# Attention scores of two heads as two 64-row products in two PSUM banks instead of one zero-padded 128-row product

## The chip, the cores and the metric

One core of a Trainium2 chip. The metric is the device time of one execution in microseconds. Before the change the median of three runs is 1158.2 us (1157.85 to 1158.86).

## What is computed

Three transformer blocks on one sequence of 256 tokens, width 1024, batch 1, all in float32. Layer 0 mixes tokens by two kinds of attention, layer 1 by a third; both end in a SwiGLU feed-forward. The third block (a gated linear recurrence) is not touched. Every score below is a product over a head dimension of 64:

```python
# layer 0, stick-breaking attention: 8 heads, each with its own key
z = einsum('bqhd,bshd->bhqs', qb, k) * scale
log_keep = where(past, log_sigmoid(-z), 0.0)
suffix = cumsum(log_keep, axis=3, reverse=True) - log_keep
w = where(past, exp(log_sigmoid(z) + suffix), 0.0)
# layer 0, gathered attention: 4 index heads pick 64 keys for each query, 8 heads share one key
logits = einsum('bqhe,bse->bhqs', qib, k_idx) * IDX_DIM ** -0.5
score = einsum('bhqs,bqh->bqs', relu(logits), wb)
_, sel = top_k(score, topk)
s = einsum('bqhd,bqkd->bhqk', qb, k[sel]) * d ** -0.5      # then softmax, times v[sel]
# layer 1, differential attention: 8 heads, two score maps each
s = einsum('bqhcd,bshcd->bhcqs', qb, k) * d ** -0.5
p = softmax(where(causal, s, -inf))
a = p[:, :, 0] - lam * p[:, :, 1]
```

## The kernel before

Activations lie transposed, features on the 128 partitions and tokens along the free axis. Weights stream from HBM by SyncE in slabs of 1 MB. ACT rounds each slab to a high part, `whi`, DVE subtracts for a low part, `wlo`, and a projection product is three PE products of 128x256 (`mm3`). The first seven slabs of layer 0 stay whole and are multiplied as float32.

No instruction is issued where it is written. The class `Plan` records every operation (`record`), `order` (line 259) lays them out on a modelled clock, with a cost for each from `cost` (line 181), a due time from the place in the text plus a bias, and buffers from fixed sets (`BUFS`); `issue` then emits them (all at line 433, so the profile shows that one line). Each engine executes its list in that order. Attention is written as generators, of which `spin` takes a step between projections, so that the planner mixes their operations into the projections.

Two heads share a 128-partition tile, one on rows 0 to 63, one on rows 64 to 127. To get both heads' scores in one product, one operand is padded: the key (layers 0's shared key in `kz_d` and `kz_i`, layer 1's in `kzt`) or the query (stick-breaking, `qz`) is laid out twice as wide, with the other head's rows zero, after a memset by GpSimd (POOL). One product over all 128 rows then gives a bank of both heads' scores, side by side:

```python
T.matmul(o, qi[:, c * S + t * 128:c * S + t * 128 + 128], two(kz_i)[:, :, :nk], start=True, stop=True)
```

`t` is the block of 128 queries; it sees `nk` = 128 or 256 keys, so such a product has 256 or 512 columns. There are 4 in `gen_topk` (index scores), 8 in `gen_dsa`, 8 in `gen_sb` (512 and 256 columns), 16 in `gen_diff`. A mask is added by a bfloat16 product with the identity (`identb`). Softmax (`softmax_pair`), exponentials and relu read the bank; probabilities are transposed by PE (`ps_t`) and multiplied by the values (`ps_o`). In `gen_sb` the values' products write 64 rows for each of two heads, on the two halves of the array's columns. `do_sb` copies queries from PSUM into `qz`, the loop over `h` in layer 1 writes q and k by additions (rotary embedding).

Of the kernel before, what the change touches and what calls it, by code (L numbers as in the profile page):

```python
# [59 lines left out]
BUFS = {'w4': 19, 'w2': 5, 'w1': 11, 'sm': 16, 'stage': 3, 'mst': 3, 'whi': 6, 'wlo': 6}  # L60
# [45 lines left out]
class Plan:  # L106
# [74 lines left out]
    def cost(self, eng, op, writes, reads):  # L181
# [255 lines left out]
def kernel(ctx, tc, io, out):  # L437
# [261 lines left out]

    def root(dst, eps, src=None):  # L700
# [253 lines left out]
    kz_t = w4("kzt")  # L954
    kz_d = kz_t[:, 0:512]
    kz_i = kz_t[:, 512:1024]
    G.memset(kz_t[:, 0:1024], 0.0)
# [6 lines left out]
    for a, kz, r0 in ((0, kz_d, 0), (1, kz_i, 64)):  # L964
        for b in range(2):
            V.tensor_add(kz[b * 64:b * 64 + 64, b * S:(b + 1) * S], t1[r0:r0 + 64, 0, :], t2[r0:r0 + 64, 0, :])
# [18 lines left out]
    def gen_topk():  # L985
        for t in range(2):
            nk = 128 * (t + 1)
            s = bias[:, t, :]
            for c in range(2):
                ps = bank("ps_i")  # L990
                o = two(ps[:, :2 * nk])
                T.matmul(o, qi[:, c * S + t * 128:c * S + t * 128 + 128], two(kz_i)[:, :, :nk], start=True, stop=True)
                r = two(w2("rl")[:, :2 * nk])
                A.activation(r, o, AF.Relu)
                for a in range(2):
                    if c == 0 and a == 0:
                        V.tensor_scalar(s[:, :nk], r[:, 0, :], wix[:, t, 0:1], 0.0, op0=ALU.mult, op1=ALU.add)
                    else:
                        V.scalar_tensor_tensor(s[:, :nk], r[:, a, :], wix[:, t, 2 * c + a:2 * c + a + 1], s[:, :nk],
# [48 lines left out]
    def gen_dsa():  # L1048
        for t in range(2):
            nk = 128 * (t + 1)  # L1050
            PT = [w4c(f"pt{t}{i}", S) for i in range(t + 1)]
            for j in range(4):
                ps = bank("ps_i")
                o = two(ps[:, :2 * nk])
                T.matmul(o, qd[j // 2][:, (j % 2) * S + t * 128:(j % 2) * S + t * 128 + 128], two(kz_d)[:, :, :nk],
                         start=True, stop=False)
                T.matmul(o, identb, biasb[:, t, None, :nk].to_broadcast([128, 2, nk]), start=False, stop=True)
                e = two(w2("e"))
                ls = softmax_pair(e, o, nk)
                for a in range(2):  # L1060
                    if a < EACT:
                        A.activation(e[:, a, :nk], e[:, a, :nk], AF.Copy, scale=ls[:, a:a + 1])
                    else:
                        V.tensor_scalar(e[:, a, :nk], e[:, a, :nk], ls[:, a:a + 1], None, op0=ALU.mult)
                for st in range(t + 1):
                    pt = bank("ps_t")
                    for a in range(2):
                        T.transpose(pt[:, a * 128:a * 128 + 128], e[:, a, st * 128:st * 128 + 128], ident)
                    A.activation(PT[st].rearrange("p j (a q) -> p a j q", a=2)[:, :, j, :], two(pt[:, :256]), AF.Copy)
                yield  # L1070
# [11 lines left out]
    qz = [w4("qz0"), w4("qz1")]  # L1082
    ks = w4c("ksb", S)
    for i in range(2):
        G.memset(qz[i], 0.0)

    def do_sb():
        for i in range(2):
            ps = two(next_pair())
            for c in range(2):  # L1090
                for a in range(2):
                    A.activation(qz[i][a * 64:a * 64 + 64, c * 512 + a * S:c * 512 + a * S + S], ps[a * 64:a * 64 + 64, c, :],
                                 AF.Copy, scale=0.125)
# [30 lines left out]
    def gen_sb():  # L1124
        for j in range(4):
            qzj = two(qz[j // 2][:, (j % 2) * 512:(j % 2) * 512 + 512])
            za, zb = bank("ps_z"), bank("ps_z")
# [743 lines left out]
```

## Time and profile before

| | |
|---|---|
| median of three runs | 1158.2 us |
| the profiled execution | 1161.21 us, span 1159.4 us |
| PE, DVE, ACT, POOL busy | 1127.6, 912.1, 723.1, 12.4 us |
| PE instructions | 8787 products, 8787 weight loads |
| mean granted PE clock | 0.99 |
| read from HBM | 229.81 MB |

The profile takes one execution apart. Busy time is the union of an engine's instructions; for the PE the ends are modelled, since products overlap in its pipeline, so prices are taken from the distance between starts. In a row's form, 128*128 says how many rows and columns of the array the instruction uses, 128x256 the output. A float32 product shows as two instructions. "Idle before" and the name behind it tell what released the engine. PEld is the weight load that belongs to a product.

### The profile page before, as it was taken

The page shows a single profiled execution, that of the slowest core. Times are in us where ns is not written, and L with a number is a line of the kernel's source. Part 1 is how long each engine was busy: PE and PEld are TensorE (multiplying, and loading weights), DVE is VectorE, ACT ScalarE, POOL GpSimd, SP SyncE. Part 2 cuts the span into 40 slices and gives each one's busy share as a digit, 9 for nine tenths or more (in the row PEclk, how much of TensorE's full clock was granted, in tenths as well). Part 3 has the DMA queues.
Part 4 walks back from the last instruction along what each step waited for, and adds up shares of the span by engine and source line. Part 5 has one row for each costly group of instructions (what it writes and reads, how often), then busy time and mean ns, then how long its engine had stood idle before and what let it go on. Part 6 is the DMA issues. An engine that isn't in the chain of part 4 may idle for free.

```text
span 1159.4 us, 21967 instructions
## 1 busy us (share of the span) xinstructions
PE 1127.6 (97%) x8787; PEld 1079.3 (93%) x8787; DVE 912.1 (79%) x1764; ACT 723.1 (62%) x1314; POOL 12.4 (1%) x18
## 2 busy tenths in 40 slices
PE   5999999999999899999999999999999999999997
PEld 4886799999998779999999999999999999999996
DVE  6799899888989899995557696996579886767652
ACT  3558677444459987764445377876757765555541
POOL 1010000000010000000000000000000000000000
PEclk9999999999999999999999999999999998999998
DMA  9938748998983244585554524344433434555441
GB/s 349 411 125 316 258 146 326 331 338 308 338 327 121 87 168 146 200 309 183 178 200 168 198 82 173 120 165 156 180 110 124 168 110 146 207 187 184 169 164 37
DMA packets 42247, 232.27 MB, mean 200 GB/s; under 512 B 4641, under 2 KB 6177, under 8 KB 24097
## 3 DMA queue, kind: packets, MB, share of 16 engines
q1 hardware_dynamic: 42144, 230.87, 54.9%
q8 instruction: 69, 1.13, 0.4%
q14 instruction: 34, 0.27, 0.1%
HBM read 229.81 MB, written 1.05 MB: 199 GB/s over the span
## 4 chain that ended last, share of the span: by engine, by line
PE 82%; DVE 9%; ACT 5%; DMA 3%; issue 1%; SPq 0%; DVEq 0%; ACTq 0%
PE pa L433 82%; DVE w L433 5%; ACT w L433 4%; DMA mst<-in_wmod_dram 2%; DVE wlo L433 2%; DVE mst L433 1%; ACT whi L433 1%; DVE sm L433 1%; DMA w<-in_pos_dram 1%; DMA w<-in_xT_dram 1%; DVE stage L433 0%; SPq L433 0%; ACT sm L433 0%; DVE mw L433 0%; DVEq L1867 0%
## 5 line engine op out<-in xcount | busy, mean ns | idle before, releaser
L433 PE MATMUL pa<-w,whi 128*128 128x256 f32 (+4 forms) x5104 | 920.3, 288 | 9.3 <-DMA whi<-in_w_dram 7.4
L433 PEld LDWEIGHTS pa<-w,whi 128*128 128x128 f32 x5104 | 771.2, 190 | 18.5 <-ACT w L433 6.7
L433 PE MATMUL pa<-w,wlo 128*128 128x256 f32 (+3 forms) x2608 | 665.7, 290 | 2.2 <-DVE wlo L433 2.2
L433 ACT ACTIVATE whi<-stage 128x1024 fp32r<-128x1024 f32 (+1 forms) x330 | 338.7, 1041 | 254.8 <-PE pa L433 226.6
L433 PEld LDWEIGHTS pa<-w,wlo 128*128 128x128 f32 x2608 | 467.2, 190 | 9.0 <-DVE wlo L433 4.0
L433 DVE TENSOR_TENSOR wlo<-stage,whi 128x1024 fp32r<-128x1024 f32 (+1 forms) x330 | 392.8, 1201 | 93.1 <-ACT whi L433 90.8
L433 ACT ACTIVATE w<-w 128x256 fp32r<-128x256 f32 (+9 forms) x257 | 117.1, 468 | 71.6 <-DVE w L433 68.0
L433 DVE TENSOR_TENSOR w<-w,w 128x256 fp32r<-128x256 f32 (+6 forms) x323 | 144.8, 465 | 10.9 <-ACT w L433 9.0
L433 ACT ACTIVATE w<-pa 128x256 f32<-128x256 f32 (+12 forms) x298 | 108.0, 390 | 47.1 <-PE pa L433 41.4
L433 DVE SCALAR_TENSOR_TENSOR mst<-mst,scb 128x1024 f32<-128x1024 f32 x90 | 108.7, 1221 | 9.2 <-DMA mst<-in_wmod_dram 8.9
L433 DVE TENSOR_TENSOR w<-w,pa 128x256 f32<-128x256 f32 (+2 forms) x146 | 58.7, 418 | 56.7 <-PE pa L433 52.0
L432 ACT ACT_TABLE_LOAD x61 | 78.3, 1283 | 1.8 <-PEq L1861 0.7
L433 PE MATMUL pa<-w,w 128*128 128x128 f32 (+8 forms) x340 | 68.6, 334 | 3.0 <-issue 1.6
L433 PEld LDWEIGHTS pa<-w,w 128*128 128x128 f32 (+4 forms) x340 | 41.9, 174 | 13.1 <-issue 7.1
L433 PE MATMUL pa<-cst,w 128*128 128x1 f32 (+4 forms) x236 | 38.8, 255 | 3.3 <-ACT w L433 3.3
L433 PEld LDWEIGHTS pa<-cst,w 128*128 128x128 f32 (+2 forms) x236 | 29.0, 158 | 10.0 <-ACT w L433 6.1
L433 PE MATMUL pa<-w 128*128 128x128 f32 x240 | 34.6, 275 | 0.0
L433 PE MATMUL pa<-whi,w 128*128 128x512 f32 x96 | 32.6, 423 | 0.0
L433 PEld LDWEIGHTS pa<-w 128*128 128x128 f32 x240 | 31.3, 191 | 0.0
L433 DVE SCALAR_TENSOR_TENSOR w<-pa,vec,w 128x256 f32<-128x256 f32 (+1 forms) x48 | 23.1, 483 | 6.6 <-PE pa L433 5.7
L433 DVE SCALAR_TENSOR_TENSOR w<-pa,mod,w 128x256 f32<-128x256 f32 x32 | 15.0, 481 | 14.8 <-PE pa L433 14.8
L433 DVE COPY_PREDICATED w<-msk,pa 128x512 f32<-128x512 uint8 x28 | 20.5, 737 | 3.9 <-PE pa L433 3.8
(144 smaller groups left out, 478.1 us busy)
## 6 DMA issues: line engine op xcount, KB each, us to landing
mst<-in_wmod_dram SPq DMA_DIRECT2D x90, 512.0 KB, 5.5
stage<-in_wgu_dram SPq DMA_DIRECT2D x44, 1024.0 KB, 5.0
stage<-in_wi_dram SPq DMA_DIRECT2D x36, 1024.0 KB, 4.8
stage<-in_wup_dram SPq DMA_DIRECT2D x22, 1024.0 KB, 4.8
stage<-in_wd_dram SPq DMA_DIRECT2D x24, 896.0 KB, 4.5
stage<-in_w_dram SPq DMA_DIRECT2D x15, 1024.0 KB, 6.7
stage<-in_wo_dram SPq DMA_DIRECT2D x12, 1024.0 KB, 4.8
stage<-in_wd_dram SPq DMA_DIRECT2D x12, 1024.0 KB, 5.4
```

The lines of the kernel that those rows point to most:

```text
L432: self.nc.scalar.preload_act_table_set(tables[i])
L433: fn(*[real(a) for a in args], **{k: real(a) for k, a in kw.items()})
```

## The change

The padding goes. Query and key of a pair of heads lie on the same rows, and a helper issues one product of 64 rows for each head, into two banks, for each of two column parts `c`; a bank now holds two scores of heads on the same rows. `gen_diff` treats two heads together: its bank holds the same score map of heads `h` and `h + 1`. The padded tiles and their memsets are dropped, `w2` gets a sixth buffer, and the planner's cost of a float32 product of 64 rows is halved.

```diff
-BUFS = {'w4': 19, 'w2': 5, 'w1': 11, 'sm': 16, 'stage': 3, 'mst': 3, 'whi': 6, 'wlo': 6}
+BUFS = {'w4': 19, 'w2': 6, 'w1': 11, 'sm': 16, 'stage': 3, 'mst': 3, 'whi': 6, 'wlo': 6}
...
-                return max(214.0, 4 * n / 2.4 + 5)
+                return max(214.0, 4 * n / 2.4 + 5) / (2 if reads[0].shape[0] == 64 else 1)
...
+    def scores(o, c, left, right, stop=False):
+
+        for a in range(2):
+            r = slice(a * 64, a * 64 + 64)
+            T.matmul(o[a][:, c, :], left[r], right[r], start=c == 0, stop=stop, skip_group_check=True)
...
-    kz_t = w4("kzt")
-    kz_d = kz_t[:, 0:512]
-    kz_i = kz_t[:, 512:1024]
-    G.memset(kz_t[:, 0:1024], 0.0)
+    kz_d, kz_i = w2("kd2")[:, :S], w2("ki2")[:, :S]
...
             for c in range(2):
-                ps = bank("ps_i")
-                o = two(ps[:, :2 * nk])
-                T.matmul(o, qi[:, c * S + t * 128:c * S + t * 128 + 128], two(kz_i)[:, :, :nk], start=True, stop=True)
+                scores(o, c, qi[:, c * S + t * 128:c * S + t * 128 + 128], kz_i[:, :nk], c == 1)
+            for a in range(2):
                 r = two(w2("rl")[:, :2 * nk])
-                A.activation(r, o, AF.Relu)
+                A.activation(r, o[a], AF.Relu)
...
+            for i in range(2):
+                o = [two(bank("ps_i")[:, :2 * nk]) for _ in range(2)]
+                for c in range(2):
+                    scores(o, c, qd[i][:, c * S + t * 128:c * S + t * 128 + 128], kz_d[:, :nk])
+                es = []
                 for a in range(2):
...
+                    T.matmul(o[a], identb, biasb[:, t, None, :nk].to_broadcast([128, 2, nk]), start=False, stop=True,
+                             skip_group_check=True)
+                    e = two(w2("e"))
+                    ls = softmax_pair(e, o[a], nk)
...
-    qz = [w4("qz0"), w4("qz1")]
-    ks = w4c("ksb", S)
-    for i in range(2):
-        G.memset(qz[i], 0.0)
+    qs, ks = w4c("qsb", S), w4c("ksb", S)
...
-            ps = two(next_pair())
-            for c in range(2):
-                for a in range(2):
-                    A.activation(qz[i][a * 64:a * 64 + 64, c * 512 + a * S:c * 512 + a * S + S], ps[a * 64:a * 64 + 64, c, :],
-                                 AF.Copy, scale=0.125)
+            ps = next_pair()
+            A.activation(qs[:, 2 * i:2 * i + 2, :], two(ps), AF.Copy, scale=0.125)
...
+            z = [bank("ps_z") for _ in range(2)]
+            for a in range(2):
+                r = slice(a * 64, a * 64 + 64)
+                T.matmul(z[a][:, 0:256], ks[r, j, 0:128], qs[r, j, :], start=True, stop=False, skip_group_check=True)
+            for a in range(2):
+                r = slice(a * 64, a * 64 + 64)
+                T.matmul(z[a][:, 256:384], ks[r, j, 128:256], qs[r, j, 128:256], start=False, stop=False, skip_group_check=True)
...
-    def gen_diff(h, q, kz):
+    def gen_diff(h, qk):
...
+            o = [two(bank("ps_i")[:, :2 * nk]) for _ in range(2)]
+            for c in range(2):
+                scores(o, c, qk[c][:, 0, t * 128:t * 128 + 128], qk[c][:, 1, :nk])
...
         if ps is not None:
             t1, t2 = rope_parts(two(ps), 2)
-            parts = [(t1[:, c, :], t2[:, c, :]) for c in range(2)]
+            V.tensor_add(qk, t1, t2)
...
-        V.tensor_add(q, parts[0][0], parts[0][1])
-        for a in range(2):
-            V.tensor_add(kz[a * 64:a * 64 + 64, a * S:a * S + S], parts[1][0][a * 64:a * 64 + 64],
-                         parts[1][1][a * 64:a * 64 + 64])
-        bg.append((gen_diff(h, q, kz), BIAS["diff"]))
+        if h % 2 == 0:
+            qk0 = qk
+        else:
+            bg.append((gen_diff(h - 1, (qk0, qk)), BIAS["diff"]))
```

What the planner makes of it is seen in the PE's order. First, the gathered attention's first pair of heads, first block of queries. Before, one product (`pa_691`, of key `w_10_413` and query `w_15_504`) among the projection's (`pa_676`), and its mask:

```order
L433 MATMUL pa_676<-w_5_351,whi_484 128x256
L433 MATMUL pa_691<-w_10_413,w_15_504 128x256
L433 MATMUL pa_676<-w_4_338,wlo_494 128x256
L433 MATMUL pa_676<-w_6_360,whi_484 128x256
L433 LDWEIGHTS identb_141
L433 MATMUL pa_691<-biasb_670,identb_141 128x256
```

After, four products of 64 rows (banks `pa_679` for rows 0 to 63, `pa_682` for rows 64 to 127) among the projection's (`pa_668`):

```order
L433 MATMUL pa_679<-w_4_448,w_12_492 128x128
L433 MATMUL pa_668<-w_5_351,whi_482 128x256
L433 MATMUL pa_682<-w_4_448,w_12_492 128x128
L433 MATMUL pa_668<-w_4_338,wlo_499 128x256
L433 MATMUL pa_679<-w_4_448,w_12_492 128x128
L433 MATMUL pa_668<-w_4_338,whi_482 128x256
L433 MATMUL pa_682<-w_4_448,w_12_492 128x128
L433 MATMUL pa_668<-w_5_351,whi_482 128x256
```

Between any two of the four stands a projection product, so no two of them are neighbours. Second, the values' products of the third stick-breaking pair. Before, the four products of the pair (`pa_1195`) stand together among the output projection's:

```order
L433 MATMUL pa_1162<-w_2_893,whi_904 128x256
L433 MATMUL pa_1195<-w_6_1183,w_3_968 64x256
L433 MATMUL pa_1195<-w_6_1183,w_3_968 64x128
L433 MATMUL pa_1195<-w_6_1183,w_3_968 64x256
L433 MATMUL pa_1195<-w_6_1183,w_3_968 64x128
L433 MATMUL pa_1107<-w_4_1068,whi_712 128x256
```

After, the same four (`pa_1183`):

```order
L433 MATMUL pa_1180<-w_0_925,whi_881 128x256
L433 MATMUL pa_1183<-w_7_1172,w_1_973 64x256
L433 MATMUL pa_1183<-w_7_1172,w_1_973 64x128
L433 MATMUL pa_1180<-w_18_898,wlo_958 128x256
L433 MATMUL pa_1183<-w_7_1172,w_1_973 64x256
L433 MATMUL pa_1183<-w_7_1172,w_1_973 64x128
L433 MATMUL pa_1180<-w_18_898,whi_881 128x256
```

One projection product now parts the first head's two from the second head's; the fourth pair is parted in the same way. Third, layer 1's heads 4 and 5, where the first block's four products stay together (`pa_4609` rows 64 to 127, `pa_4611` rows 0 to 63):

```order
L433 MATMUL pa_4609<-w_5_4516 128x128
L433 MATMUL pa_4611<-w_5_4516 128x128
L433 MATMUL pa_4609<-w_5_4516 128x128
L433 MATMUL pa_4611<-w_5_4516 128x128
L433 LDWEIGHTS identb_140
L433 MATMUL pa_4611<-causb_211,identb_140 128x256
```

where there stood, for each head, one product and its mask (here head 0's, `pa_4246`, behind a projection):

```order
L433 MATMUL pa_4194<-w_3_3990,wlo_4198 128x256
L433 MATMUL pa_4194<-w_3_3990,whi_4159 128x256
L433 MATMUL pa_4246<-w_2_4074,w_4_4222 128x256
L433 LDWEIGHTS identb_141
L433 MATMUL pa_4246<-causb_211,identb_141 128x256
```

The two heads' scores are now computed at one place, both row halves side by side in the list.

## Rows read from the trace of the kernel before

**Rows 1.** The page's first part: busy us (share of the span) and instructions of each engine.
```profile
PE 1127.6 (97%) x8787; PEld 1079.3 (93%) x8787; DVE 912.1 (79%) x1764; ACT 723.1 (62%) x1314; POOL 12.4 (1%) x18
```
**Rows 2.** The page's fourth part: the chain of work that ended last, share of the span by engine.
```profile
PE 82%; DVE 9%; ACT 5%; DMA 3%; issue 1%; SPq 0%; DVEq 0%; ACTq 0%
```
**Rows 3.** Busy time by stretch: start and end in us, length, then busy us and instructions of each engine, granted PE clock, share of the DMA engines, GB/s.
```profile
core 0: us, PE busy (x) PEld busy (x) DVE busy (x) ACT busy (x) POOL busy (x), PEclk, DMA share, GB/s
54.00:76.50 22.50, 22.50 (x107) 19.24 (x106) 20.44 (x70) 14.32 (x25) 1.86 (x4) 1.00 0.34 132
76.50:119.00 42.50, 39.40 (x193) 26.20 (x193) 40.61 (x81) 32.38 (x86) 1.09 (x1) 1.00 0.82 295
119.00:145.00 26.00, 24.97 (x188) 21.96 (x186) 22.27 (x53) 17.02 (x31) 0.00 (x0) 1.00 0.72 247
366.00:400.00 34.00, 29.39 (x199) 24.12 (x199) 29.25 (x67) 32.93 (x76) 0.00 (x0) 1.00 0.31 113
400.00:436.00 36.00, 35.54 (x192) 27.97 (x190) 34.52 (x93) 29.25 (x92) 0.00 (x0) 1.00 0.42 147
```
**Rows 4.** Groups of equal instructions, shapes kept apart: the padded score products. Count, then busy us and mean ns of one, then idle time before them.
```profile
L433 PE MATMUL pa<-w,w 128*128 128x512 f32 x36 | 18.6, 599 | 0.0
L433 PE MATMUL pa<-w,w 128*128 128x256 f32 x36 | 11.2, 392 | 2.6 <-issue 1.6 <-DVE w L433 1.0
```
**Rows 5.** PE in order of time around two padded products (`w,w`): start us, length us, form, count of instructions merged into the row.
```profile
59.73 1.02 PE L433 MATMUL pa<-w,w 128*128 128x512 f32 x2
60.58 1.03 PE L433 MATMUL pa<-w,wlo 128*128 128x256 f32 x4
...
82.53 0.59 PE L433 MATMUL pa<-w,w 128*128 128x256 f32 x2
82.96 0.27 PE L433 MATMUL pa<-biasb,identb 128*128 128x256 bf16 x1
```
**Rows 6.** PE in order of time around the gathered attention's values product, first block: two heads on two halves of the columns.
```profile
93.74 0.40 PE L433 MATMUL pa<-wlo,w 128*128 128x512 f32 x1
94.07 1.08 PE L433 MATMUL pa<-w,w 128*64 128x512 f32 x4
95.08 0.44 PE L433 MATMUL pa<-cst,w 128*128 128x128 f32 x2
```
**Rows 7.** PE in order of time around the values product of one stick-breaking pair (`w,w`), between products of the output projection.
```profile
120.64 0.64 PE L433 MATMUL pa<-w,whi 128*128 128x256 f32 x4
121.11 0.28 PE L433 MATMUL pa<-w,wlo 128*128 128x256 f32 x1
121.32 0.88 PE L433 MATMUL pa<-w,w 128*64 128x256 f32 x8
122.12 0.50 PE L433 MATMUL pa<-w,whi 128*128 128x256 f32 x2
122.47 0.40 PE L433 MATMUL pa<-w,wlo 128*128 128x256 f32 x2
122.70 0.28 PE L433 MATMUL pa<-w,whi 128*128 128x256 f32 x1
```
**Rows 8.** PE in order of time around a small float32 product on a corner of the array, in the third block.
```profile
776.78 0.52 PE L433 MATMUL pa<-w,whi 128*128 128x258 f32 x3
777.23 0.40 PE L433 MATMUL pa<-w,w 32*32 32x128 f32 x2
777.56 0.51 PE L433 MATMUL pa<-w,wlo 128*128 128x258 f32 x2
777.91 0.28 PE L433 MATMUL pa<-w,whi 128*128 128x258 f32 x1
```
**Rows 9.** What the PE waited for between 76.5 and 145 us: us in total, times, longest.
```profile
PE pa L433 <- DVE w L433: 2.3, 2, 1.2
PE pa L433 <- ACT w L433: 1.5, 1, 1.5
PE pa L433 <- DVE biasb L433: 0.3, 1, 0.3
```
**Rows 10.** PE in order of time: the starts behind the two longest of these waits, a transpose of probabilities and stick-breaking's cumulative sum.
```profile
84.75 0.33 PE L433 MATMUL pa<-cst,w 128*128 128x128 f32 x1 [1.51 <-ACT w L433]
...
117.39 0.70 PE L433 MATMUL pa<-w,cst 128*128 128x512 f32 x1 [1.22 <-DVE w L433]
```
**Rows 11.** What the PE waited for between 366 and 436 us, layer 1's attention.
```profile
PE pa L433 <- DVE wlo L433: 1.6, 3, 0.8
PE pa L433 <- issue: 1.6, 1, 1.6
PE pa L433 <- DVE w L433: 1.0, 2, 0.7
PE pa L433 <- ACT w L433: 0.8, 1, 0.8
```
**Rows 12.** Groups of equal instructions, shapes kept apart: additions on DVE by width, and copies from PSUM on ACT.
```profile
L433 DVE TENSOR_TENSOR w<-w,w 128x256 f32<-128x256 f32 x99 | 40.9, 422 | 3.3 <-ACT w L433 2.4
L433 DVE TENSOR_TENSOR w<-w,w 128x512 f32<-128x512 f32 x49 | 32.6, 687 | 2.7 <-ACT w L433 2.7
L433 DVE TENSOR_TENSOR w<-w,w 64x256 f32<-64x256 f32 x20 | 8.3, 417 | 0.3
L433 ACT ACTIVATE w<-pa 128x512 f32<-128x512 f32 x22 | 12.7, 597 | 11.3 <-PE pa L433 11.3
L433 ACT ACTIVATE w<-pa 64x256 f32<-64x256 f32 x8 | 3.0, 378 | 2.5 <-PE pa L433 2.5
```

More of the change, by code (lines that the diff above doesn't have):

```diff
@@ L965 @@
         for b in range(2):
[L966 removed]
+            V.tensor_add(kz[b * 64:b * 64 + 64, :], t1[r0:r0 + 64, 0, :], t2[r0:r0 + 64, 0, :])
     A.activation(vx, ps[:, S:], AF.Copy)
@@ L1125, in gen_sb @@
         for j in range(4):
-            qzj = two(qz[j // 2][:, (j % 2) * 512:(j % 2) * 512 + 512])
-            za, zb = bank("ps_z"), bank("ps_z")
-            T.matmul(two(za), ks[:, j, 0:128], qzj, start=True, stop=False, skip_group_check=True)
-            T.matmul(two(zb[:, :256]), ks[:, j, 128:256], qzj[:, :, 128:256], start=True, stop=False, skip_group_check=True)
-            for ap in (two(za)[:, :, 0:128], two(zb[:, :256])):
-                T.matmul(ap, identb, strib[:, None, :].to_broadcast([128, 2, 128]), start=False, stop=True,
-                         skip_group_check=True)
@@ new lines, in gen_sb @@
+            for a in range(2):
+                r = slice(a * 64, a * 64 + 64)
+                T.matmul(z[a][:, 0:256], ks[r, j, 0:128], qs[r, j, :], start=True, stop=False, skip_group_check=True)
+            for a in range(2):
+                r = slice(a * 64, a * 64 + 64)
+                T.matmul(z[a][:, 256:384], ks[r, j, 128:256], qs[r, j, 128:256], start=False, stop=False, skip_group_check=True)
+            sp = two(w4("sp")[:, :768])
+            for a in range(2):
+                T.matmul(z[a][:, 0:512].rearrange("p (b n) -> p b n", b=2)[:, :, 0:128], identb,
+                         strib[:, None, :].to_broadcast([128, 2, 128]), start=False, stop=True, skip_group_check=True)
+                A.activation(sp[:, a, :], z[a][:, :384], AF.Abs)
@@ L1140, in gen_sb @@
+            A.activation(sp, sp, AF.Exp, scale=-1.0)
+            A.activation(sp, sp, AF.Ln, bias=1.0)
+            for a in range(2):
+                V.scalar_tensor_tensor(sp[:, a, :], z[a][:, :384], 0.0, sp[:, a, :], op0=ALU.max, op1=ALU.add)
             yield
-            T.matmul(za, C("tn"), sp[:, 0:512], start=False, stop=False, skip_group_check=True)
-            T.matmul(two(za)[:, :, 128:256], C("neg1"), two(sp[:, 512:768]), start=False, stop=True, skip_group_check=True)
-            T.matmul(zb[:, :256], C("tn"), sp[:, 512:768], start=False, stop=True, skip_group_check=True)
@@ L1145, in gen_sb @@
             w = w4("wsb")
-            A.activation(w[:, 0:512], za, AF.Exp)
-            A.activation(w[:, 512:768], zb[:, :256], AF.Exp)
+            for a in range(2):
+                T.matmul(z[a][:, :384], C("tn"), sp[:, a, :], start=False, stop=False, skip_group_check=True)
+                T.matmul(z[a][:, 128:256], C("neg1"), sp[:, a, 256:384], start=False, stop=True, skip_group_check=True)
+                A.activation(w[:, a * 384:a * 384 + 384], z[a][:, :384], AF.Exp)
             yield
@@ L1280 @@
             ps = gemm_pair(X)
[L1281 removed]
         if h % 2 == 0:
[L1283 to L1284 removed]
+            aTt, kzt = w4("aT"), w4("qk")
         aT[h] = aTt[:, (h % 2) * 384:(h % 2) * 384 + 384]
[L1286 removed]
+        qk = two(kzt[:, (h % 2) * 512:(h % 2) * 512 + 512])
         if ps is not None:
             t1, t2 = rope_parts(two(ps), 2)
[L1289 removed]
+            V.tensor_add(qk, t1, t2)
         else:
[L1291 removed]
             for c in range(2):
                 t1, t2 = rope_parts(pss[2 * (h - 2) + c][:, None, :], 1)
[L1294 to L1299 removed]
+                V.tensor_add(qk[:, c, :], t1[:, 0, :], t2[:, 0, :])
+        if h % 2 == 0:
+            qk0 = qk
+        else:
+            bg.append((gen_diff(h - 1, (qk0, qk)), BIAS["diff"]))
         if h >= 2:
```

84 lines of the change are left out of this document (32 added, 52 removed).

## Prediction

> **What bounds the kernel now.** I read the busy line first: TensorE (PE) is busy 97% of the span, VectorE (DVE) 79%, ScalarE (ACT) 62% [rows 1]. The chain that ended last says the same in another way: 82% of it is PE, 9% DVE, 5% ACT, 3% DMA [rows 2]. So whatever adds to the PE's work in a stage where the PE seldom waits adds to the end, nearly one for one. The stages that the change touches are then read by stretch [rows 3]. From 54 to 76.5 us, where the index scores stand among the products of the unsplit weights, the PE is busy 22.50 of 22.50 us. From 76.5 to 119 us, the gathered and the stick-breaking attention, it is busy 39.40 of 42.5, but DVE is too, 40.61. In layer 1's attention the picture differs: ACT is busy 32.93 of 34.0 us at first, then DVE 34.52 of 36.0, while the PE has 4.6 us free in the first half. The granted clock is 1.00, the 2.4 GHz level, in all five, so no clock term stands in the sum.
>
> **What a padded product costs.** There are 36 of them, each two instructions in the trace: 18 of 512 columns and 18 of 256 [rows 4]. A mean there is a pipelined duration (599 and 392 ns), not a price; the price is the distance to the next start. One of 512 columns starts at 59.73 and its follower at 60.58: 0.85 us. One of 256 starts at 82.53, its follower at 82.96: 0.43 us [rows 5]. Together 18 x 0.85 + 18 x 0.43 = 23.0 us, all on the PE. Half of it multiplies zeros. Were the two heads always to run side by side, 11.5 us would go.
>
> **What the change makes of them.** 72 products of 64 rows take their place, 36 of 128 columns and 36 of 256; the columns add up to the same. A gain comes only where a product on rows 0 to 63 and one on rows 64 to 127 stand in the same stretch of the PE's order, nothing of full size between them. In the order of the changed program the 72 stand in 40 such stretches. 24 of the 40 hold a single product, with full-size products before and behind it, as in the order's first piece above; there nothing overlaps. The other 16 hold 48 products.
>
> For the price of such a stretch the trace has neighbours: products that use half of the array's columns (128*64) or a corner of it (32*32), among full-size ones.
> - Side by side: in the stretch at 94.07 two fp32 products of 512 columns, four instructions, lie on the two halves of the columns. One after the other they would take 2 x 0.85 = 1.71 us. The next start is at 95.08, 1.01 us on: the halves did run together [rows 6].
> - The edge: full-size products follow each other every 0.12 us (122.47 to 122.70, two of them). From 120.64 to 122.47 there are seven, 0.83 us, and the stretch at 121.32. It cost 1.83 - 0.83 = 1.00 us, of which streaming, two halves together, is (0.43 + 0.21) = 0.64. The edge is 0.36 us [rows 7]. From 776.78 to 777.91 stand five full-size products, 0.59 us, and one small fp32 product of 128 columns, 0.21 us: the edge is 0.33 us [rows 8].
> - Where it lies: the engine stops about 0.1 us before and 0.1 us behind the stretch, and each time a weight load is no longer hidden. Behind it the second start comes after 0.35 us (122.12 to 122.47) in place of 0.235: 0.115 us for a load of 128 columns. The neighbours load 64 and 32 columns on the way in; the new products load 128, which adds 0.05 and 0.08 us. Both rows give the same **0.41 us per stretch**.
>
> **The sum on the PE.** Taking the larger of the two row halves in each stretch, streaming falls by 0.64 us in the index scores, 1.28 in the gathered attention, 1.71 in stick-breaking and 3.41 in layer 1: 7.0 us of the 11.5. The 40 edges cost 16.4 us: 6 in the index scores, 20 in the rest of layer 0, 14 in layer 1. And the probabilities-times-values products of two stick-breaking pairs, which stood as one stretch of four, are cut in two by a projection product (the order's second piece): two more edges, and the two halves of 0.64 us no longer overlap, 2 x (0.36 + 0.64) = 2.0 us. By stage: index scores +1.8, the rest of layer 0 2.99 saved against 8.2 + 2.0, so +7.2, layer 1 +2.3. **The PE gets 11.4 us more to do, not less.**
>
> **What of it reaches the end.** Index scores: no PE wait there, +1.8 in full. Rest of layer 0: the PE waits 4.1 us for DVE and ACT between 76.5 and 145 [rows 9], the longest at 84.75 and at 117.39, where it has run out of projection work [rows 10]. More PE work ahead shortens a wait only if what is waited for does not itself start later; some of it hangs on scores that do. Bounds: 0 to 4.1 us hidden. I take the middle, 2.0, so +5.2. Layer 1: the PE waits 5.0 us there [rows 11], ACT and DVE are full; +2.3 is hidden, and if that cover is gone it costs 2.3.
>
> **DVE, ACT and the rest.** Layer 1 writes q and k straight: 8 adds of 128x256 and 16 of 64x256 become 6 of 128x512 and 4 of 128x256. That is 8 x 0.42 + 16 x 0.42 = 10.0 us against 6 x 0.69 + 4 x 0.42 = 5.8: 4.2 us off DVE [rows 12]. The stick-breaking queries leave PSUM by two copies of 128x512 in place of eight of 64x256: 1.2 for 3.0 us off ACT [rows 12]. Softmax, exponentials, transposes and bias products keep count and size. The memsets that go were POOL's, busy 12.4 us in all [rows 1]. In layer 1's first half ACT is the fuller engine and is not relieved; in its second half DVE is. I take this at nothing, bounds -2.0 (half of 4.2) to 0. A pair of heads now holds two PSUM banks and starts when both are ready, so it may come later; that is in the upper end. DMA moves the same bytes; the planner shifts a few modulation loads by some places.
>
> Sum: 1.8 + 5.2 + 0 + 0 = **+7.0 us**. The profiled execution took 1161.2 us (span 1159.4); it stands 3.0 above the median of the three runs, 1158.2. So 1168.2 by its own time, **1165.2 us** as a median. Low bound of this case: 1.8 + (7.2 - 4.1) - 2.0 = +2.9, 1161.1; high bound: +11.4, 1169.6.
>
> **The rivals.**
> - *The row halves run one pass at a time.* An fp32 product is two passes, written as both passes of one head, then both of the other. If starts keep strictly to that order, only the second pass of the first overlaps the first pass of the second: at most half of the 7.0 us, +3.5; with no overlap at all +7.0. That gives 1165.2 + 3.5 to 1165.2 + 7.0, about 1170. For it: no row here shows two row halves. Against: in rows 6 two column halves of the same kind took 1.01 us, where three passes of 0.43 would take 1.28. The Trainium skill has the rule (TensorE: Matmul & The Clock Gate, Part 3: Packing small matmuls, where matmuls start and end strictly in program order); by it the sum is +10.5, by the row +7.0, and the row disagrees with it for column halves. Chance 0.18.
> - *DVE and ACT set the time, and the PE's extra work is hidden.* If layer 0's attention waits on DVE, 40.61 of 42.5 us busy, the edges fall into waits and the relief in layer 1 counts. The point where this decides: the PE's free time in 76.5 to 145 would have to be at least the 7.2 us added. It is 3.1 + 1.0 in rows 3, which speaks against. It would give 1.8 - 2.0, about 1158. Chance 0.12: no change 0.09, faster 0.03.
> - *Faster: a change between row sizes costs nothing.* If a stretch of 64-row products needs no stop of the array and its weight loads stay hidden, the 40 edges vanish. Then the sum is -7.0 + 2.0 - 2.0 = -7.0, 1151.2; with all pairs side by side as well, -11.5, 1146.7. It decides below 7.0 / 40 = 0.18 us per edge. The Trainium skill speaks for that side (TensorEngine Tiling (Array Packing), Overview: contraction of at most 64 rows, up to twice as fast); by it the time would be the 1146.7. Against: every stretch of another size in the trace has its edge, 0.33 and 0.36 us in rows 7 and 8. Chance 0.08.
> - The forecast itself: 0.62.
>
> **How the numbers follow.** A change of 0.2%, 2.3 us, is about what a measurement of this kernel can tell from none: 1155.9 to 1160.5. Slower takes the forecast and the first rival, 0.80, less 0.02 for the low tail of the forecast: 0.78. Same: 0.09 + 0.02 = 0.11. Faster: 0.08 + 0.03 = 0.11. The range reaches from the edge of the second rival, 1158.5, to the high end of the first, 1172.2 (+14.0); it leaves out the fast rival and part of the second.
>
> **What would show it.** In the changed kernel's profile: (1) PE rows of the form 64*128, 144 instructions; (2) where two such products of different halves stand together, starts a few ns apart, else the first rival holds; (3) about 0.1 us between the end of streaming and the start of such a stretch, and 0.35 us between the first two full-size starts behind it, else the third rival; (4) PE waits in 76.5 to 145 us below 4.1 us, and the output projection's first product some 6 to 9 us later than now; (5) DVE's 64x256 adds down from 20 to 4. The prediction is wrong if the stage up to about 145 us is not longer, or if layer 1's attention loses more than 2.3 us, which would be late starts of the pairs.

## The result, and the profile after

| | kernel before | changed kernel |
|---|---|---|
| median of 4 runs | 1158.03 us (1156.31 to 1158.86) | 1164.91 us (1164.55 to 1165.24) |
| ratio, 95% interval | | 1.0066, 1.0053 to 1.0079 |
| predicted | | 1165.2, range 1158.5 to 1172.2 |
| the profiled execution, its span | 1161.21 us, 1159.4 | 1164.85 us, 1162.9 |

Slower by 6.9 us by the medians, where 7.0 was forecast. The ratio is worked out from all runs and is not the quotient of the two medians; by it the loss is 7.6 us. A second measurement (the run e10 below) gave 1.0078, 1.0062 to 1.0094, so +9.0. The number was right. Of its terms one was wrong, and another came out right with parts that did not, as the experiments show.

The page's busy line and chain of the changed kernel, which answer [rows 1, 2]:

```profile
PE 1135.5 (98%) x8867; PEld 1082.3 (93%) x8867; DVE 908.7 (78%) x1750; ACT 722.5 (62%) x1308; POOL 4.7 (0%) x11
...
PE 90%; DVE 4%; ACT 4%; DMA 1%; issue 0%; SPq 0%; DVEq 0%; ACTq 0%
```

The PE is busy 7.9 us longer and is on 90% of the chain instead of 82%. DVE is busy 3.4 us less. POOL, without the memsets of the padded tiles, is busy 4.7 us instead of 12.4. The groups of equal instructions show the new products, 144 instructions of the form 64*128, in place of [rows 4], and the adds and copies that answer [rows 12]: DVE's 64x256 adds fall from 20 to 4, ACT's copies of 64x256 are gone.

```profile
L433 PE MATMUL pa<-w,w 64*128 64x256 f32 x40 | 9.0, 423 | 0.0
L433 PE MATMUL pa<-w 64*128 64x256 f32 x32 | 8.2, 432 | 1.0 <-DVE w L433 1.0
L433 PE MATMUL pa<-w,w 64*128 64x128 f32 x40 | 8.0, 310 | 0.3 <-DVE w L433 0.3
L433 PE MATMUL pa<-w 64*128 64x128 f32 x32 | 4.6, 314 | 1.5 <-DVE w L433 0.9 <-ACT w L433 0.5
...
L433 DVE TENSOR_TENSOR w<-w,w 128x512 f32<-128x512 f32 x55 | 36.7, 686 | 1.2 <-ACT w L433 0.9
L433 DVE TENSOR_TENSOR w<-w,w 64x256 f32<-64x256 f32 x4 | 1.7, 420 | 0.1
```

The PE in order of time in the index scores of the changed kernel (start us, length us, form, count merged into the row):

```profile
55.86 0.48 PE L433 MATMUL pa<-w,w 64*128 64x128 f32 x2
56.28 0.70 PE L433 MATMUL pa<-w,whi 128*128 128x256 f32 x2
56.91 0.48 PE L433 MATMUL pa<-w,w 64*128 64x128 f32 x2
...
58.38 0.70 PE L433 MATMUL pa<-w,w 64*128 64x256 f32 x2
59.01 0.70 PE L433 MATMUL pa<-w,wlo 128*128 128x256 f32 x2
59.64 0.70 PE L433 MATMUL pa<-w,w 64*128 64x256 f32 x2
60.27 0.70 PE L433 MATMUL pa<-w,wlo 128*128 128x256 f32 x2
60.89 0.70 PE L433 MATMUL pa<-w,w 64*128 64x256 f32 x4
61.53 1.78 PE L433 MATMUL pa<-w,wlo 128*128 128x256 f32 x7
```

Both disputed prices can be read here. **The edge:** from 58.38 to 59.64 stand a lone product of 64 rows and one of full size, each 256 columns in two passes and so 0.43 us by [rows 5]: 0.86 us in 1.26, an edge of 0.40. From 55.86 to 56.91 it is 0.21 + 0.43 in 1.05: 0.41. **The overlap:** the stretch at 59.64 holds one product (two instructions) and the next start comes 0.63 us later; the one at 60.89 holds two, on the two row halves, and takes 0.64. The second was free: the four instructions start at 60.894, 60.900, 61.214 and 61.220.

To place the 6.9 us I cut each trace at the same pieces of projection work: at the starts of the 61st, 181st, 781st, 2221st, 2821st, 4201st and 6601st product that reads a weight chunk (whi or wlo). Every kernel here has 7,856 of them. The first stretch shown holds the index scores, the second the rest of layer 0's attention, the third layer 1's attention. A row gives length, busy us of each engine, granted clock; the PE's free time is length minus busy. Before:

```profile
35.63:65.76 30.13, 29.78 (x135) 25.24 (x134) 24.75 (x56) 20.43 (x39) 1.50 (x2) 1.00 0.82 326
65.76:185.68 119.92, 115.30 (x763) 97.32 (x762) 112.89 (x262) 84.63 (x184) 1.44 (x2) 1.00 0.64 229
358.14:471.46 113.32, 108.26 (x754) 95.23 (x753) 105.45 (x256) 94.63 (x234) 0.00 (x0) 1.00 0.40 141
635.77:999.97 364.20, 362.66 (x2942) 355.21 (x2940) 283.99 (x519) 253.09 (x427) 1.34 (x1) 0.98 0.41 147
```

After:

```profile
35.42:67.67 32.25, 31.59 (x143) 24.94 (x142) 26.90 (x65) 19.63 (x36) 0.63 (x2) 1.00 0.82 328
67.67:192.40 124.73, 122.49 (x804) 101.90 (x802) 110.42 (x247) 81.89 (x178) 1.44 (x2) 0.99 0.60 211
364.94:480.53 115.59, 111.67 (x786) 97.83 (x785) 106.65 (x254) 96.21 (x242) 0.00 (x0) 0.99 0.44 156
645.12:1003.49 358.37, 357.48 (x2941) 350.81 (x2940) 284.38 (x519) 253.06 (x427) 0.98 (x1) 0.99 0.42 149
```

Index scores +2.1 us, rest of layer 0 +4.8, layer 1 +2.3: 9.2 us in the three. (The stretches between and behind them, 781st to 2221st and 2821st to 4201st, agree within 0.3 us.) The fourth row, stages that the change doesn't touch, shows why the two profiled executions are only 3.6 us apart: this execution of the kernel before spent more of it at the lower clock, 0.98 against 0.99, and took 5.8 us longer there.

### The profile page after: what moved, and what is told of

Its sections match the earlier page's. It is cut to its first block, busy times and chain, and to the rows that moved or that the text cites. A ratio compares the mean times of both kernels' runs of the same rounds, so it can differ in the third digit from the quotient of the medians.

```text
span 1162.9 us, 22115 instructions
## 1 busy us (share of the span) xinstructions
PE 1135.5 (98%) x8867; PEld 1082.3 (93%) x8867; DVE 908.7 (78%) x1750; ACT 722.5 (62%) x1308; POOL 4.7 (0%) x11
## 3 DMA queue, kind: packets, MB, share of 16 engines
HBM read 229.81 MB, written 1.05 MB: 199 GB/s over the span
## 4 chain that ended last, share of the span: by engine, by line
PE 90%; DVE 4%; ACT 4%; DMA 1%; issue 0%; SPq 0%; DVEq 0%; ACTq 0%
PE pa L433 90%; ACT w L433 3%; DVE w L433 3%; DMA whi<-in_w_dram 1%; DVE wlo L433 0%; DVE sm L433 0%; ACT whi L433 0%; SPq L433 0%; DVE stage L433 0%; ACT sm L433 0%; DVEq L1868 0%; DVE cosT L433 0%; DVE lam L433 0%; ACT lam L433 0%; DVE lnv0lfg L433 0%
## 5 line engine op out<-in xcount | busy, mean ns | idle before, releaser
L433 DVE TENSOR_TENSOR w<-w,w 128x256 fp32r<-128x256 f32 (+7 forms) x309 | 141.1, 472 | 9.2 <-ACT w L433 7.3
L433 ACT ACTIVATE w<-pa 128x256 f32<-128x256 f32 (+11 forms) x292 | 106.6, 392 | 52.7 <-PE pa L433 47.2
L433 PE MATMUL pa<-w,w 128*128 128x128 f32 (+8 forms) x348 | 57.6, 306 | 0.7 <-DVE w L433 0.3
L433 PEld LDWEIGHTS pa<-w,w 128*128 128x128 f32 (+5 forms) x348 | 40.1, 171 | 12.6 <-issue 5.4
L433 PE MATMUL pa<-w 128*128 128x128 f32 (+2 forms) x304 | 46.7, 295 | 2.5 <-DVE w L433 1.9
L433 PEld LDWEIGHTS pa<-w 128*128 128x128 f32 (+1 forms) x304 | 37.8, 190 | 6.2 <-issue 3.8
L433 DVE SCALAR_TENSOR_TENSOR w<-pa,mod,w 128x256 f32<-128x256 f32 x32 | 15.1, 481 | 13.3 <-PE pa L433 13.2
```

Of the source, the lines that this page charges most:

```text
L433: fn(*[real(a) for a in args], **{k: real(a) for k, a in kw.items()})
```

## Experiments

Length in us of the three attention stretches by the profile of each run, the median time, and the ratio to the kernel before on the same chip. Where a difference below has a ratio behind it in brackets, it is worked out from the ratio, else from medians or stretches.

| run | index | rest of layer 0 | layer 1 | median us | ratio (95%) |
|---|---|---|---|---|---|
| before | 30.13 | 119.92 | 113.32 | 1156.3 to 1158.0 in five sets | 1 |
| changed kernel | 32.25 | 124.73 | 115.59 | 1164.9 | 1.0066 (1.0053 to 1.0079) |
| e10, changed kernel again | 32.25 | 124.72 | 115.56 | 1166.5 | 1.0078 (1.0062 to 1.0094) |
| e1, 40 zero products, 128 rows | 30.13 | 121.54 | 113.45 | 1169.1 | 1.0094 (1.0075 to 1.0112) |
| e2, 40 zero products, 64 rows | 30.13 | 122.72 | 113.64 | 1186.2 | 1.0247 (1.0227 to 1.0267) |
| e3, layer 0 alone | 32.25 | 126.34 | 116.04 | 1168.9 | 1.0093 (1.0075 to 1.0112) |
| e4, layer 1 alone | 30.14 | 119.69 | 115.44 | 1160.9 | 1.0028 (1.0013 to 1.0042) |
| e5, pairs and values together | 29.66 | 122.76 | 118.54 | 1167.4 | 1.0090 (1.0077 to 1.0103) |
| e6, pairs together | 29.66 | 126.99 | 114.08 | 1165.6 | 1.0079 (1.0062 to 1.0096) |
| e7, another price | 32.26 | 143.00 | 125.08 | 1196.4 | 1.0346 (1.0330 to 1.0363) |
| e8, order of after, 128 rows | 30.75 | 121.20 | 115.61 | 1161.2 | 1.0032 (1.0021 to 1.0043) |
| e9, order of e5, 128 rows | 30.17 | 123.04 | 118.66 | 1166.3 | 1.0075 (1.0059 to 1.0090) |
| e11, before with w2 = 6 | 30.14 | 122.78 | 114.87 | 1161.8 | 1.0042 (1.0030 to 1.0055) |
| e12, before, padded price halved | 30.14 | 120.60 | 116.71 | 1160.2 | 1.0024 (1.0014 to 1.0034) |

### The edge by itself: e1 and e2

In the kernel before, inside layer 0's down projection, where the PE never waits:

```diff
                 for k in range(c3 * 8, min(NF, c3 * 8 + 8)):
+                    if k % 4 == 3 and zeros_left[0]:
+                        zeros_left[0] -= 1
+                        T.matmul(ps[:, 0:128], zed[0:64], X[0][k][0:64, 0:128].bitcast(F32), start=False, stop=False,
+                                 skip_group_check=True)      # e1: zed[0:128], X[0][k][0:128, 0:128]
```

> The kernel before, with 40 extra products in layer 0's down projection (5 in each of its 8 sums): a 128x128 block of zeros times 128 columns of the gate, fp32, 128 rows, two instructions each. They add nothing but time. This is the control for the next run. At the streaming price of such a product, half of the 0.43 us that the 256-column one took, each theory expects 40 x 0.213 = +8.5 us against the kernel before, about 1166.5 us; without edges, since all products there have 128 rows.

> The same kernel and the same order of instructions as the run with the 128-row zero products; each of the 40 products reads rows 0 to 63 alone. Nothing stands beside them in the other half. Theory A (a stretch of 64-row products among products of 128 rows costs an edge of 0.41 us, whatever the attention does): +8.5 + 40 x 0.41 = +24.9 us against the kernel before, about 1183; 16.4 us above the control. Theory B (the edges of the changed kernel are waits and a worse order of the attention, and the change of row size costs nothing): the same as the control, +8.5 us. Between 2 and 14 us above the control the edge would be real and smaller here than I priced it.

The stretch of the down projection (781st to 2221st product, 172.46 us before: 185.68 to 358.14), first of e1, then of e2:

```profile
186.87:368.30 181.43, 181.43 (x1542) 181.43 (x1541) 159.27 (x272) 87.09 (x136) 3.70 (x4) 1.00 0.88 315
```
```profile
188.19:385.18 196.99, 196.99 (x1542) 186.78 (x1541) 159.84 (x272) 87.35 (x136) 3.75 (x4) 1.00 0.81 290
```

The control costs 181.43 - 172.46 = 8.97 us, 0.224 per product; 8.5 was expected. The same order with 64 rows costs 15.56 us more, **0.39 us per stretch**, expected 0.41. The medians say 17.2 us, 0.43. The edge is real, belongs to the change of row size, and needs neither attention nor a wait. (The control's median is 3.5 us above what was expected; 1.6 of that is in layer 0's attention.)

That surplus says something about the table. The zero products come at 280 us and later. e2 has the order of e1, instruction for instruction, and yet the rest of its layer 0, long before the first zero product, took 122.72 us against 121.54. So in this stretch a difference of 1.2 us between two profiles needs no change of the order; e11 below shows where it can come from.

### One layer at a time: e3 and e4

e3 takes the layer 0 functions of the changed kernel with `gen_diff` and its caller from before; e4 the reverse. Both keep the sixth buffer of `w2` and the halved price.

> The change in layer 0 alone; layer 1's attention pads as before. 26 stretches of 64-row products instead of 40. By the sum: streaming 3.6 us less, 26 edges of 0.41 us = 10.7, the cut values products 2.0: +9.0 us on PE, of which 2.0 was put down as hidden: +7.0 us, about 1165. The trace of the changed kernel showed +6.7 at 178 us, with one stretch of half clock in it that took some 1.7 us: by that reading +5.0. Rival (the loss is spread over both layers, late starts of the pairs in layer 1): +4 or less here, and the rest in the run with layer 1 alone.

> The change in layer 1 alone; layer 0 pads as before. 17 stretches: streaming 3.2 us less, 17 edges 7.0 us: +3.8 us on PE. The prediction put such a sum down as hidden by PE waits there (0 us); if that cover is gone, +3.8. With the 4.2 us of relief on DVE reaching the end by half, -2.0. The trace of the changed kernel showed +2.3 at 450 us, of which 1.7 stood in a stretch of half clock. I expect 0 to +2 us, 1158 to 1160.

Both missed, and the parts don't add up: +10.8 us (1.0093) where 5 to 7 were expected and +3.2 (1.0028) where it was 0 to 2, together 14, for a change of 7 to 9. In e3 the layer 1 stretch lost 2.7 us with the padded products of before in it. Something other than the products was costing time. Its rest of layer 0, in the same order as in the changed kernel, was also 1.6 us longer, with the clock at 0.97 in place of 0.99.

### Fewer stretches: e5, e6, e7

e5 hands the planner one operation for the four score products of a pair, and one for the values products; e6 does so for the scores alone; e7 leaves the operations as they are and changes one line of the planner's costs, which e5 and e6 change too.

```diff
+    def together(self, outs, calls):      # e5, e6: several matmuls, one operation in the order
+        ...
-            scores(o, c, qk[c][:, 0, t * 128:t * 128 + 128], qk[c][:, 1, :nk])
+            scores(o, [qk[c][:, 0, t * 128:t * 128 + 128] for c in range(2)], [qk[c][:, 1, :nk] for c in range(2)])
...
-                return max(214.0, 4 * n / 2.4 + 5) / (2 if reads[0].shape[0] == 64 else 1)
+                return max(214.0, 4 * n / 2.4 + 5) + (410.0 if reads[0].shape[0] == 64 else 0.0)    # e5, e6, e7
```

> The changed kernel with the planner given one operation for the four score products of a pair of heads (two columns sets on each row half), one for the four of a stick-breaking pair, and one for its four values products, so that nothing of full size comes between them. 18 stretches of 64-row products in place of 40, all with the two halves side by side, and the values products in the 5 stretches that they had before the change. Theory A (time = streaming + 0.41 us per stretch): 23.0 us of padded streaming becomes 11.5, edges 18 x 0.41 = 7.4: -4.1 us on PE against the kernel before; of this 2.3 us in layer 0, where PE sets the time, and 1.8 in layer 1, where it waits anyway: 1154 to 1156. Theory B (two PSUM banks per pair, or the late starts of pairs, cost the time, not the edges): still at or above the changed kernel, 1164 or more, since a pair now also waits for all four operands.

> As the run before, but the four values products of a stick-breaking pair are left for the planner to place one by one. 18 stretches of 64-row products again (-4.1 us), but the values products now lie in 10 stretches instead of 5, three pairs of halves apart: 5 x 0.36 + 3 x 0.64 = +3.7 us. Theory A: -0.4 us on PE against the kernel before, 1156 to 1159, and 2 to 4 us above the run with the values products together. Theory B (the edges don't matter): no difference between the two.

> The changed kernel with one line different: the planner's cost of a 64-row product is the full streaming plus 410 ns instead of half the streaming. The products themselves are the same; only the order moves. In that order there are 48 stretches instead of 40: streaming 6.4 us less than padded, edges 19.7, cut values products 2.0: +15.3 us on PE against the kernel before, 3.9 more than the changed kernel's 11.4. Theory A: slower than the changed kernel by 2 to 4 us, 1167 to 1169. Rival (the planner's halved price is what spoiled the order, and a true price mends it): back to 1158 to 1161.

All three missed. In the index scores, where the PE sets the time, e5 and e6 did what the sum says: -0.47 us against before, from 2 x (0.43 + 0.21) - 2 x 0.41 = 0.46 saved. Elsewhere it was lost again. e5's third stretch, then the PE in order of time inside it (line 441 of that kernel is line 433 of the others):

```profile
360.63:479.17 118.54, 107.49 (x786) 97.50 (x785) 107.81 (x254) 94.97 (x235) 0.00 (x0) 0.96 0.45 157
```
```profile
375.33 0.39 PE L441 MATMUL pa<-w,whi 128*128 128x256 f32 x2
384.83 0.45 PE L441 MATMUL pa<-cst,w 128*128 128x128 f32 x1 [9.11 <-DVE w L441]
...
387.21 0.41 PE L441 MATMUL pa<-w,wlo 128*128 128x256 f32 x1
387.42 0.63 PE L441 MATMUL pa<-w,whi 128*128 128x256 f32 x2
...
390.91 0.40 PE L441 MATMUL pa<-w,whi 128*128 128x256 f32 x2
391.14 0.28 PE L441 MATMUL pa<-w,wlo 128*128 128x256 f32 x1
```

The PE is busy 0.8 us less than before, and the stretch is 5.2 us longer. It stands 9.1 us in front of a transpose whose input DVE is late with, and has no projection product placed there. Behind that wait its products start every 0.21 us (387.21 to 387.42) until about 390.4, then every 0.12 (391.14 less 390.91, two products): first the lower level of the clock, 1.2 GHz, then the upper. e7's rest of layer 0 is the same in a larger measure: 143.00 us, 13.3 of them free, granted clock 0.93. An order chosen with a truer price was some 30 us worse than one with a wrong price.

### The change without its row halves: e8 and e9, beside e10

The costs that the planner sees stay, so every engine has the changed kernel's order, instruction for instruction:

```diff
-            r = slice(a * 64, a * 64 + 64)
-            T.matmul(o[a][:, c, :], left[r], right[r], start=c == 0, stop=stop, skip_group_check=True)
+            T.matmul(o[a][:, c, :], left, right, start=c == 0, stop=stop, skip_group_check=True)
```

> The changed kernel with its order kept instruction for instruction (the planner gets the same costs), but each of the 72 score products reads all 128 rows instead of 64, so that it mixes both heads' scores: this is for its time alone. All the structure of the change stays (two PSUM banks per pair, fewer adds and copies, cut values products); what goes is the change of row size and the overlap of the row halves. Theory A (row-size edges 40 x 0.41 = 16.4 us against 7.0 us of overlap): PE work 9.4 us less than the changed kernel, of which 1.8 in the index scores, 5.2 in the rest of layer 0 and 2.3 in layer 1; 5 to 9 us faster than the changed kernel, 1156 to 1160. Theory B (the structure costs the time: pairs that start later, banks, order): within 2 us of the changed kernel, or slower by the lost overlap, up to 7 us.

> The kernel with the four score products of a pair together and the values products together, its order kept instruction for instruction, but each score product reads all 128 rows (both heads mixed, for its time alone). PE work: 11.5 us of overlap lost, 18 edges of 0.41 = 7.4 won: +4.1 us. If PE work set that kernel's time, it would be 4 us slower than it, 1171. If waits of PE for DVE and ACT and the half-clock stretches behind them set it (its trace: PE waits 9.3 us for DVE in layer 1, granted clock 0.71 and 0.78 in 376 to 396 us), more PE work falls into the waits: within 1.5 us of it, 1166 to 1169, or faster by up to 3 where a half-clock stretch goes.

> The changed kernel itself, for comparison on the same chip with the runs beside it: 1165 us, +7 us against the kernel before.

Neither theory alone. e8 took 1161.2 us, 5.2 less than the changed kernel beside it and 3.7 more than before. So of the 9.0 us in this set, **5.2 are the row halves** (edges less overlap, and what the clock did with them) **and 3.7 the rest of the change** (its order, the cut values products, the banks, and the moments at which its loads land). e8's second and third stretch, then one short window at the end of stick-breaking in e8:

```profile
66.21:187.41 121.20, 117.45 (x804) 102.97 (x802) 110.89 (x254) 81.67 (x178) 1.45 (x2) 1.00 0.61 217
359.95:475.56 115.61, 109.63 (x786) 99.94 (x785) 106.68 (x254) 96.21 (x242) 0.00 (x0) 1.00 0.44 156
```
```profile
110.00:119.00 9.00, 9.00 (x50) 6.18 (x49) 7.68 (x13) 4.97 (x11) 0.00 (x0) 1.00 0.78 264
```

The same window in the changed kernel with one in layer 1's attention, and the PE's two waits in the first:

```profile
110.00:119.00 9.00, 7.54 (x27) 4.34 (x26) 8.31 (x15) 6.71 (x17) 0.00 (x0) 0.81 0.78 288
376.00:396.00 20.00, 18.04 (x122) 14.90 (x121) 17.34 (x42) 19.59 (x51) 0.00 (x0) 0.91 0.33 119
```
```profile
112.65 0.73 PE L433 MATMUL pa<-cst,w 128*128 128x128 f32 x3 [0.78 <-ACT w L433]
114.06 0.44 PE L433 MATMUL pa<-cst,w 128*128 128x128 f32 x2 [0.68 <-ACT w L433]
```

Stretch by stretch, changed kernel less e8: index +1.5; rest of layer 0 +3.5, of which (1 - 0.81) x 9 = 1.7 is the lower clock in the first window; layer 1 0.0, though the clock took up to (1 - 0.91) x 20 = 1.8 us there. e10, the changed kernel again, shows both windows alike (0.82 and 0.91).

The 5.2 may be too low. At the first product of the output projection (the 321st that reads a weight chunk) e8 is at 116.64 us, the changed kernel at 123.23. Then DVE in e8 stands 2.95 us in front of a modulation load (`mst`) that has not landed, and the PE behind it 1.53 us for DVE. In the changed kernel, later by then, DVE stands 0.50 us there and the PE does not wait.

e9 against e5 is the counterpart. By the sum e9 has 4.1 us more PE work; its three stretches took 0.9 us more, and its median, on another chip, is 1.2 us lower. That fits extra work which falls into waits, as expected there.

### The order alone: e11 and e12

The kernel before with its padded products. e11 changes one number, e12 the price that the planner sees; the instructions are the same, in another order, but for two more loads of an ACT table in e12.

```diff
-BUFS = {'w4': 19, 'w2': 5, ...
+BUFS = {'w4': 19, 'w2': 6, ...                                  # e11
...
-                return max(214.0, 4 * n / 2.4 + 5)
+                return max(214.0, 4 * n / 2.4 + 5) / (2 if self.half else 1)     # e12: half is set around the padded products
```

> The kernel before with one number of the change, the sixth buffer of the tag w2. Padded products stay; the instructions are the same, and the planner puts them in another order. Theory C (some 2 to 4 us of the change come from the new order and not from the products: with all 72 products at 128 rows the changed order was 3.7 us slower than before, 2.3 of it in layer 1's attention; and with padded products there, the run of layer 0 alone lost 2.7 us in that stage as well): any new order that wasn't tuned costs this, +2 to +4 us here. Theory D (the order as such costs nothing; it is the cut values products, 2.0 us, and the pairs that wait for two banks): the same as before within 1.5 us.

> The kernel before with the padded score products' cost in the planner halved, as the changed kernel halves that of its 64-row products. Products, banks and adds are those of before; only the order moves. Theory C: +2 to +4 us. Theory D: the same as before within 1.5 us.

Both slower than before, +4.9 us (1.0042) and +2.8 (1.0024), with no product changed. The two that the change itself brings, a sixth buffer and a halved price, each reorder the program, and either program loses about as much as all of e8.

The order is not shown to be the whole cause. e11 loses 2.9 us in the rest of layer 0 and 1.6 in layer 1. But e4 has the same buffers and the same padded layer 0, and up to about 345 us each of its engines has e11's order, instruction for instruction; its rest of layer 0 took 119.69 us, e11's 122.78. What differs in that stretch is how long DVE stands in front of modulation loads (`mst`), and the PE behind DVE. First e4, then e11 (us in total, times, longest):

```profile
DVE mst L433 <- DMA mst<-in_wmod_dram: 3.4, 4, 1.4
PE pa L433 <- DVE w L433: 1.7, 2, 1.1
```
```profile
DVE mst L433 <- DMA mst<-in_wmod_dram: 7.3, 4, 3.3
PE pa L433 <- DVE w L433: 4.5, 3, 2.2
```

So e11's loss in layer 0 came with loads that landed later, in an order that e4 ran without loss. Why they landed later, no run tells. In layer 1 neither engine waits for a load, in the kernel before, e11 or e12; there no other cause than the order is seen for e11's 1.6 us (with a lower clock, 0.91 in 376 to 396 us, before 1.00) and e12's 3.4. e12's second and third stretch:

```profile
65.52:186.12 120.60, 116.77 (x764) 98.86 (x763) 110.16 (x258) 84.92 (x184) 1.45 (x2) 0.99 0.63 221
358.69:475.40 116.71, 109.85 (x755) 95.28 (x754) 107.81 (x261) 97.64 (x236) 0.00 (x0) 1.00 0.43 146
```

Layer 1 is 3.4 us longer than before; the PE is free 6.9 us there instead of 5.1, and of this it waits 4.2 us for ACT, before 0.8.

## Why the prediction was right, point by point

- **The price of a stretch.** 0.41 us, from neighbours that used parts of the columns. In the changed trace 0.40 and 0.41; by itself 0.39 (e2). Right at these places, and it was the step on which the sign hung; the average over the attention came out lower (below).
- **Side by side.** Two halves in 0.64 us where one takes 0.63: the first rival falls. The Trainium skill (TensorE: Matmul & The Clock Gate, Part 3: Packing small matmuls), by which matmuls start and end in program order, would have made that stretch one pass, 0.21 us, longer, if each pass counts as a matmul, as the first rival read it. The trace disagrees with that reading for row halves too; whether it also disagrees by whole products, it does not show, since the records don't say which pass is whose.
- **The third rival,** that a change of row size costs nothing, decided below 0.18 us per edge; e2 has twice that. The doubling in the Trainium skill (TensorEngine Tiling (Array Packing), Overview) is there for the streaming alone, as the 0.64 us show; with 24 of 40 stretches holding one product it was not to be had.
- **Index scores:** +1.8 forecast in full, +2.1 measured; +1.5 of it by e8 is the row halves.
- **Rest of layer 0:** +5.2 forecast, +4.8 measured. That they agree is partly luck, since the parts came out otherwise. Edges less overlap were put at 5.2 us of PE work and 2.0 hidden. Against e8 the PE is busy 5.0 us longer, 1.7 of it the lower clock, so 3.3 of work; its free time fell from 3.75 to 2.24, so 1.5 hidden. The lower clock, for which the sum had no term, stands in for work that was not there. The work is less than reckoned in all three stretches together: busy time less clock gives 1.5 + 3.3 + 0.2 = 5.0 us for the row halves, not 16.4 - 7.0 = 9.4. With the 7.0 of overlap as reckoned that is (5.0 + 7.0) / 40 = 0.30 per stretch and not 0.41. The 2.0 for the cut values products fits the 2.2 us by which e8 is busier there than before; that these are its cause is not shown.
- **Layer 1: the wrong term.** Forecast 0, measured +2.3. The reason given for the 0 holds: the row halves' work and even 1.8 us of lower clock vanish in PE waits, as e8 takes the same 115.6 us without them (the PE's free time is 5.98 us there, 3.92 in the changed kernel). What failed is the step "the planner shifts a few modulation loads by some places" with its relief of -2.0 to 0: a new order was priced at nothing. The stretch lost 1.6 to 3.4 us in e3, e11 and e12, where the padded products stand in it unchanged, and 2.3 in e8. The +2.3 named in the prediction for the case that the cover is gone is the same number by chance.
- **The second rival,** that DVE and ACT set the time, was given 0.12 for the whole. It is right for layer 1, and for e5 against e9; it is wrong for layer 0, where 5.0 us came through.
- **The relief:** DVE's busy time fell by 3.4 us, 4.2 forecast for layer 1 alone; none of it is seen at the end, where layer 1 got longer.
- **Waits:** below 4.1 us in 76.5 to 145, forecast; now 1.5:

```profile
PE pa L433 <- ACT w L433: 1.5, 2, 0.8
```

  The sign beside it failed: the output projection's first product came 4.2 us later (123.23 us, before 119.02), where 6 to 9 were forecast.
- **Open:** what in the re-planned programs costs their 3 to 5 us. They show it as PE waits for DVE and ACT. In layer 0 a part of it is DVE's wait for modulation loads, which differs by 3.9 us between e4 and e11 in one and the same order; no run holds these loads still, so order and loads are not told apart there, in e8 either. In layer 1 no run tells which move does it. Nor is it settled why a stretch cost 0.30 us in the attention and 0.39 among the down projection's products. One part can be read: behind a values product, which has a form of its own (128*64), the way into a stretch costs no more than the way into a full-size product, 0.52 us from start to start in both (121.08 to 121.60; in e8 114.24 to 114.76).

The 7.0 was thus 5.0 for the row halves (1.8 + 5.2 - 2.0), which measured 5.0 by the stretches and 5.2 by the medians, and 2.0 for the cut values products, where the rest of the change measured 3.7. The first term came out right, with a dearer edge and no clock in place of a cheaper edge and a lower clock, which is luck in the size, not in the sign; the second was too low by what the re-planned program lost.

## What to carry to other kernels

Products on the row halves of the array pay only where they stand side by side and their stretch saves more streaming than its 0.39 us edge: a pair of 128 float32 columns saves 0.21, one of 256 saves 0.43. Where an order is planned from costs, count the stretches in the planned order, not the products in the source. The edge was 0.39 us by itself and 0.30 on average in this attention. And price the re-planning itself: test an edit beside a run that has its order without its effect, and the old program re-planned, before crediting the edit with a few tenths of a per cent. Even the same order can differ by 3 us in one stage, as e4 and e11 do, so compare what the engines wait for before calling the order the cause.

## What was not expected of the hardware

The lower of the two clock levels (1.2 GHz) came into stages that had been at 1.00 before. With one and the same order, the window 110 to 119 us had 1.00 in e8, where the PE had no free time, and 0.81 in the changed kernel, where it had waited 0.78 and 0.68 us. In e5 products behind a wait of 9.1 us started every 0.21 us instead of every 0.12 for over 5 us. e5 has less PE work than e9 by the sum and the lower clock in the rest of layer 0, 0.97 against 1.00.

But a wait alone does not bring the lower level. The same window before, and in e11:

```profile
110.00:119.00 9.00, 7.73 (x38) 3.93 (x38) 8.48 (x18) 7.21 (x15) 0.00 (x0) 1.00 0.84 286
```
```profile
110.00:119.00 9.00, 6.63 (x34) 3.75 (x34) 8.97 (x20) 6.99 (x14) 0.00 (x0) 1.00 0.67 221
```

The PE is free 1.3 and 2.4 us there, in the kernel before with a wait of 1.22 us [rows 10], and the clock stays at 1.00. So these runs show lower clock behind some waits and not behind others, and not what decides. In stages where nothing was changed the lower level came and went between kernels, too: 364.2 us before, 358.4 after, for the same work.
